# Attention as a three-stage pipeline in fixed TensorE order, with inputs placed early and narrower key blocks at the sides

## The chip, the core and the metric

The program runs on one core of a Trainium2 chip. A core has five engines with an instruction stream each: TensorE (PE, matrix products and transposes), VectorE (DVE), ScalarE (ACT), GpSimd (POOL) and SyncE (SP, which mostly issues DMA transfers). A scheduler in the compiler sets the order of the instructions on each engine; at run time each engine takes its own in that order and waits by semaphores for the others. The metric is the time of one execution on the device in microseconds (us), the median of several runs.

## The reference

Two layers run over 1024 latent tokens (a 16 x 64 grid, width 1024) and 256 context tokens. Each layer has one input projection that feeds three parallel mixers (mLSTM, neighbourhood attention with 8 heads of 64, RG-LRU), one output projection (oproj) over their concatenation, a gated residual, and an MLP. The last layer needs no context output. What the change touches is the neighbourhood attention:

```python
def row_block(r):                       # one row of the grid, 64 queries
    sr = jnp.clip(r - wr // 2, 0, rows - wr)                # 8 key rows
    k_win = k_band[:, :, col_idx]                           # 16 key columns per query
    s_loc = einsum('bqhd,brqchd->bhqrc', q_r, k_win) * scale + bias
    s_ctx = einsum('bqhd,bkhd->bhqk', q_r, kc) * scale      # all 256 context keys
    p = softmax(concatenate([s_loc, s_ctx], axis=-1), axis=-1)
    o = einsum(p_loc, v_win) + einsum(p_ctx, vc)
y_ctx = softmax(qc @ kc * scale) @ vc                       # context tokens, first layer only
x = x + g1 * (concatenate([ym, yn, yl], axis=-1) @ w_out)
```

## The kernel before

All products are fp32 in effect: each operand is split into a high and a low part (`split`, L210 and L211; for weights `load_w`, L200 and L201), and a product is three matmuls (low-high, high-high, high-low). PSUM has 8 banks: three tagged a, two b, one each of c, p and q (`bank`).

A layer runs: input projections of mLSTM and LRU with their scans; then `na_group(0)` and `na_group(1)`, each of which projects K, Q and V for two head pairs, writes them to DRAM token by token (`u_nk`, `u_nq`, `u_nv`) and takes the norms; then the attention stage; then the second half of oproj and the MLP.

**Prep** (`na_prep(hp)`, a generator, one `yield` per step): for a head pair, loads K and Q (`ut`), scales them by their norms on DVE (L684), transposes them on PE (L692, L694), and writes high and low parts as `KH`, `KL`, `QS` (L700 to L706); four DMAs (`KH<-KH`, `KL<-KL`) and one per Q step and head (`QS<-ql`) put the halves on the other 64 partitions. The prep of head pair 0 runs after `na_group(1)`; those of 1 to 3 one step at a time in `side()`.

**Attention** (`na_att`): for each of four head pairs, two units of context queries (layer 0 only) and eight local units: a column block `b` of 16 query columns and a half `g` of 8 query rows, 128 queries, against 32 key columns and 11 (`g = 0`) or 12 (`g = 1`) key rows, 352 or 384 keys, plus 256 context keys. That makes 40 units in layer 0 and 32 in layer 1. A unit, for two heads: score matmuls (L834 local, L838 context) into three a banks; on DVE a fused bias, negation and running minimum for the local keys (L848) and the context keys (L852); Exp on ACT with the row sum into `den` (L855); `side()`; then `softmax_pv`: transposes of the weights (L727), copies of these to SBUF as `PT` (L729, L744 on ACT, L746 on DVE; where the last tile of local keys is 96 wide, three copies for each head instead of one), `den` inverted (L749), spread to 128 x 128 (L751) and transposed by PE (L753), the products with the values `VB` (local) and `VC` (context) (L757), and their scaling into `yr` (ACT copy L865, DVE multiply L866).

**Filler.** The first half of oproj (the rows of mLSTM and LRU; `fill`, `oproj`, matmuls psp at L1363) is handed out by `side()` in pieces of 12 matmuls, paced by `due`; `issue_after` holds a piece behind the scores of the unit. Its inputs `yh` are loaded by `y_load` and split; `ev_half` adds the result to the residual rows in DRAM (`xs`, L1380). Behind the attention, `y_load` and `split` bring the four attention row blocks (`yl`, and `yr` for the last head pair), and the wide oproj takes them (L1363, psa, psp and psq from `xh`, `xlo`; 288 matmuls in layer 0, 192 in layer 1), and adds to `res` (L1464), loaded by SP at L1458. Between them DVE computes modulation vectors from `mr` (L333, L342, L344).

The scheduler may move instructions of different stages past each other on every engine, within what the data, the buffers and `issue_after` allow.

## Time and profile before

| | |
|---|---|
| median of 3 runs | 3132.05 us (3132.0 to 3132.32) |
| the profiled execution | 3124.27 us, its span 3122.5 us |
| mean granted clock of PE, share of full speed | 0.988 |
| PE busy | 3020.2 us, 97% of the span |
| DVE busy | 1900.0 us, 61% |
| ACT busy | 1128.4 us, 36% |

A busy share is the share of the span in which an engine ran an instruction. The attention stage of layer 0 lies at about 510 to 755 us and its wide oproj ends near 805; in layer 1 it is 2130 to 2347, and 2386.

### The profile page before, as it was taken

The page shows a single profiled execution, that of the slowest core. Times are in us where ns is not written, and L with a number is a line of the kernel's source. Part 1 is how long each engine was busy: PE and PEld are TensorE (multiplying, and loading weights), DVE is VectorE, ACT ScalarE, POOL GpSimd, SP SyncE. Part 2 cuts the span into 40 slices and gives each one's busy share as a digit, 9 for nine tenths or more (in the row PEclk, how much of TensorE's full clock was granted, in tenths as well). Part 3 has the DMA queues.
Part 4 walks back from the last instruction along what each step waited for, and adds up shares of the span by engine and source line. Part 5 has one row for each costly group of instructions (what it writes and reads, how often), then busy time and mean ns, then how long its engine had stood idle before and what let it go on. Part 6 is the DMA issues. An engine that isn't in the chain of part 4 may idle for free.

```text
span 3122.5 us, 47474 instructions
## 1 busy us (share of the span) xinstructions
PE 3020.2 (97%) x18250; PEld 2558.1 (82%) x18250; DVE 1900.0 (61%) x4318; ACT 1128.4 (36%) x2011; POOL 291.0 (9%) x252
## 2 busy tenths in 40 slices
PE   7999998999899999999999999998899999999999
PEld 6888898778788888887778889997787777887877
DVE  5757655787977667455444574765787444444444
ACT  4632223574421222233222453234564222332222
POOL 0410000222200000010000511002222000000000
PEclk8999999999999999999999999999999999999999
DMA  9624567765233444233323632347753332333233
GB/s 272 216 73 144 171 190 199 226 169 178 68 115 105 126 124 125 75 108 101 95 88 94 175 123 82 100 131 219 219 172 110 95 95 89 99 116 91 92 96 93
DMA packets 531098, 410.73 MB, mean 132 GB/s; under 512 B 27580, under 2 KB 496536, under 8 KB 530872
## 3 DMA queue, kind: packets, MB, share of 16 engines
q1 hardware_dynamic: 519448, 387.41, 41.9%
q0 software_dynamic: 8576, 15.00, 1.5%
q10 hardware_dynamic: 2848, 5.28, 0.5%
q8 instruction: 144, 2.36, 0.3%
q14 instruction: 82, 0.67, 0.1%
HBM read 339.72 MB, written 67.53 MB: 130 GB/s over the span
## 4 chain that ended last, share of the span: by engine, by line
PE 70%; DVE 11%; DMA 10%; issue 2%; ACT 2%; SPq 1%; POOL 0%; ACTq 0%; DVEq 0%; POOLq 0%
PE psa L468 14%; PE psa L1515 13%; PE psq L468 5%; PE psp L468 5%; PE psp L1515 4%; DMA mr<-in_w_mod_dram 4%; PE psq L1515 4%; PE psp L483 4%; PE psq L483 3%; PE psp L1363 3%; DVE ma L344 3%; PE psc L757 2%; PE psb L727 1%; PE psa L1363 1%; PE psa L834 1%
## 5 line engine op out<-in xcount | busy, mean ns | idle before, releaser
L200 ACT ACTIVATE wh<-wr 128x1024 fp32r<-128x1024 f32 (+3 forms) x356 | 361.8, 1021 | 929.7 <-PE psa L1515 296.3
L201 DVE TENSOR_TENSOR wl<-wr,wh 128x1024 fp32r<-128x1024 f32 (+3 forms) x356 | 424.5, 1196 | 380.6 <-ACT wh L200 374.3
L468 PE MATMUL psa<-xlo,wh 128*128 128x512 f32 (+1 forms) x856 | 319.5, 373 | 2.2 <-DVE xlo L444 2.1
L468 PE MATMUL psa<-xh,wh 128*128 128x512 f32 (+1 forms) x856 | 318.8, 373 | 2.4 <-ACT xh L443 2.4
L468 PE MATMUL psa<-xh,wl 128*128 128x512 f32 (+1 forms) x856 | 319.3, 373 | 1.4 <-DVE wl L201 1.4
L1515 PE MATMUL psa<-hl,wh 128*128 128x512 f32 (+1 forms) x768 | 286.1, 373 | 1.3 <-DVE hl L211 1.3
L1515 PE MATMUL psa<-hh,wh 128*128 128x512 f32 (+1 forms) x768 | 284.6, 376 | 0.6 <-ACT wh L200 0.5
L1515 PE MATMUL psa<-hh,wl 128*128 128x512 f32 (+1 forms) x768 | 278.1, 373 | 0.6 <-DVE wl L201 0.6
L1519 DVE SCALAR_TENSOR_TENSOR res<-psa,modt,res 128x512 f32<-128x512 f32 (+1 forms) x192 | 130.9, 693 | 165.8 <-PE psa L1515 165.6
L468 PEld LDWEIGHTS psa<-xlo,wh 128*128 128x128 f32 x856 | 161.6, 189 | 33.4 <-DVE xlo L444 2.9
L468 PEld LDWEIGHTS psa<-xh,wh 128*128 128x128 f32 x856 | 161.5, 189 | 33.4 <-ACT xh L443 2.8
L468 PEld LDWEIGHTS psa<-xh,wl 128*128 128x128 f32 x856 | 161.6, 189 | 32.5 <-DVE wl L201 2.2
L409 POOL TENSOR_TENSOR acc<-acc,nsq 128x512 f32<-128x512 f32 (+1 forms) x56 | 80.3, 1446 | 1020.6 <-ACT nsq L408 970.7
L210 ACT ACTIVATE hh<-rl 128x512 fp32r<-128x512 f32 (+1 forms) x160 | 93.5, 589 | 225.0 <-DVE rl L1491 225.0
L1515 PEld LDWEIGHTS psa<-hh,wh 128*128 128x128 f32 x768 | 144.5, 188 | 34.8 <-ACT wh L200 8.9
L483 PE MATMUL psp<-wl,xh 128*128 128x256 f32 (+1 forms) x560 | 163.1, 291 | 5.9 <-DVE wl L201 5.8
L1515 PEld LDWEIGHTS psa<-hh,wl 128*128 128x128 f32 x768 | 144.5, 188 | 28.6 <-DVE wl L201 1.5
L1515 PEld LDWEIGHTS psa<-hl,wh 128*128 128x128 f32 x768 | 144.6, 188 | 27.8 <-DVE hl L211 1.5
L483 PE MATMUL psp<-wh,xh 128*128 128x256 f32 (+1 forms) x560 | 162.2, 290 | 2.5 <-ACT wh L200 2.4
L483 PE MATMUL psq<-wh,xh 128*128 128x256 f32 (+1 forms) x560 | 162.7, 290 | 1.4 <-ACT usq L641 0.8
L483 PE MATMUL psq<-wl,xh 128*128 128x256 f32 (+1 forms) x560 | 160.9, 287 | 0.0
L483 PE MATMUL psq<-wh,xlo 128*128 128x256 f32 (+1 forms) x560 | 160.2, 286 | 0.0
(409 smaller groups left out, 7342.4 us busy)
## 6 DMA issues: line engine op xcount, KB each, us to landing
wr<-in_w_mlp_dram SPq DMA_DIRECT2D x256, 512.0 KB
mr<-in_w_mod_dram SPq DMA_DIRECT2D x92, 512.0 KB
wr<-in_w_in_dram SPq DMA_DIRECT2D x48, 512.0 KB
tab<-T_d SPq DMA_DIRECT2D x48, 384.0 KB
T_d<-E_d POOLq DMA_DIRECT2D x48, 256.0 KB, 6.5
ab<-row_d SPq DMA_DIRECT2D x36, 256.0 KB
xT_d<-res SPq DMA_DIRECT2D x4, 2048.0 KB
wr<-in_w_out_dram SPq DMA_DIRECT2D x32, 256.0 KB
```

The source lines that it names most:

```text
L200: act.activation(hi[:, a:b], raw[:, a:b], AF.Copy)
L201: dve.tensor_sub(lo[:, a:b], raw[:, a:b], hi[:, a:b].bitcast(F32))
L210: act.activation(hi, src32, AF.Copy)
L344: dve.scalar_tensor_tensor(a, raw[:, k], s[:, k], a, op0=OP.mult, op1=OP.add)
L409: pool.tensor_add(acc[bi], acc[bi], sq[:, :n])
L468: m = pe.matmul(t[:, :n], w[a][:, k, :], X[bi][b][:, k, :], start=(i == 0), stop=(i == 23))
L483: m = pe.matmul(t[:, :cols], X[bi][b][:, half * 4 + k, o:o + P], ws[half][a][:, k, :], start=(i == 0), stop=(i == 23))
L727: pe.transpose(t[:w, j * P:(j + 1) * P], S[e][:, o:o + w], permT)
L757: pe.matmul(to[64 * e:64 * e + 64, :P], vals[i][:w, 64 * e:64 * e + 64], PT[:w, e, i], start=(i == 0), stop=(i == nt - 1))
L1363: pe.matmul(t[:, :n], w[a][:, k, cc * P:(cc + 1) * P], Y[bi][b][:, k], start=(i == 0), stop=(i == 11))
L1515: m = pe.matmul(t[:, :n], w[a][:, k, cc * P:(cc + 1) * P], H[bi, k][b], start=(i == 0), stop=(i == 3 * GH - 1))
L1519: dve.scalar_tensor_tensor(xr[bi][:, ct], t[:, :n], G2[:, ct, v:v + 1], xr[bi][:, ct], op0=OP.mult, op1=OP.add)
```

## The change

1. On PE, the instructions issued while `pinned[0]` is set, which is the whole attention stage, stay in program order. `issue_after` with the anchors is gone there.
2. `na_att` becomes `na_units`, a generator of units of three parts. One iteration of the new loop runs the scores of unit u, a slot of filler, one prep step of the next head pair, the transposes and copies of unit u-1, the values of unit u-2, and a second slot. Two more iterations drain it. The filler yields after every four matmuls instead of twelve.
3. The prep of head pair 0 runs between the Q and the V projection of `na_group(1)`. The pool of the filler's inputs (`yp`) is opened ahead of `na_group(1)`. Some buffers change: `VB` 3 to 2, `VC` 1 to 2, `xs` 3 to 2; the keys and queries of odd head pairs lie in another pool.
4. Side blocks (b = 0, 3) take 24 key columns, centre blocks 32, and all units 12 key rows: 288 or 384 local keys.
5. The transposed weights leave PSUM in three copies per local unit: 512 and 256 wide on ACT, 512 wide on DVE.
6. `rb` comes from one reciprocal of `den` broadcast to 128 x 128, instead of a reciprocal of 128 x 2 and a broadcast copy.

```diff
+    pinned = [False]
+
+    def in_order(op):
+        def issue(*a, **k):
+            ins = op(*a, **k)
+            return tc.keep_in_program_order(ins) if pinned[0] else ins
+        return issue
+
+    pe = SimpleNamespace(matmul=in_order(nc.tensor.matmul), transpose=in_order(nc.tensor.transpose))
...
-        def na_group(grp):
+        def na_group(grp, between=()):
             na_proj(grp, C_NK, u_nk[l], ALLT, nssq["k"])
             na_proj(grp, C_NQ, u_nq[l], QT, nssq["q"])
+            phase(f"na_prep{l}")
+            run(between)
+            phase(f"na_inB{l}")
             na_proj(grp, C_NV, u_nv[l], ALLT, None)
...
+        def transpose_p(npl, S, w, permT):
+
+
+            PT = npl.tile([P, 10, P], F32, name=nm("PT"), tag="PT", bufs=2)
+            tl = [(e, i * w, w) for e in range(2) for i in range(3)] if w else []
+            tl += [(e, 3 * w + i * P, P) for e in range(2) for i in range(2)]
+            o = 10 - len(tl)
+            for a, b, on_dve in ((0, 4, False), (4, 6, False), (6, 10, bool(w))):
+                if a < o:
+                    continue
                 t = bank("bbq")
-                for j, (e, i) in enumerate(gr):
-                    o, w = tiles[i]
-                    pe.transpose(t[:w, j * P:(j + 1) * P], S[e][:, o:o + w], permT)
-                if len(gr) == 2:
-                    act.activation(PT[:, :, 4], t[:, 0:2 * P].rearrange("p (k q) -> p k q", q=P), AF.Copy)
-                    continue
-                if nt == 2:
-                    act.activation(PT[:, :, 0:2], t.rearrange("p (e k q) -> p e k q", e=2, q=P), AF.Copy)
-                    continue
-                e = gi
-
-                j = 0
-                while j < 4:
-                    j2 = j
-                    w = tiles[j][1]
-                    while j2 < 4 and tiles[j2][1] == w:
-                        j2 += 1
-                    src = t[:w, j * P:j2 * P].rearrange("p (k q) -> p k q", q=P)
-                    if e == 0:
-                        act.activation(PT[:w, e, j:j2], src, AF.Copy)
-                    else:
-                        dve.tensor_copy(PT[:w, e, j:j2], src)
-                    j = j2
-
-            dve.reciprocal(den, den)
+                h = tl[a - o][2]
+                for j in range(a, b):
+                    e, c, _ = tl[j - o]
+                    pe.transpose(t[:h, (j - a) * P:(j - a + 1) * P], S[e][:, c:c + h], permT)
+                src = t[:h, 0:(b - a) * P].rearrange("p (k q) -> p k q", q=P)
+                if on_dve:
+                    dve.tensor_copy(PT[:h, a:b], src)
+                else:
+                    act.activation(PT[:h, a:b], src, AF.Copy)
+            return PT
...
+        def values_p(npl, PT, den, w, loc, vc, permT, ydst):
+
+
             rb_ = npl.tile([P, 2, 64], F32, name=nm("rb"), tag="rb", bufs=2)
-            dve.tensor_copy(rb_, den.unsqueeze(2).to_broadcast([P, 2, 64]))
+            dve.reciprocal(rb_, den.unsqueeze(2).to_broadcast([P, 2, 64]))
...
+                    cw = (24, 32, 32, 24)[b]
+                    kc = (0, 8, 24, 40)[b]
+                    to = 8 if b == 3 else 0
+                    w = 4 * cw
+                    nl = 3 * w
...
-                        nr = 11 if g == 0 else 12
-                        nl = nr * 32
...
+                                pe.matmul(tl[:, :nl].rearrange("p (r c) -> p r c", c=cw), QS[e][:, qo:qo + P],
+                                          kv[:, r0:r0 + 12, kc:kc + cw], start=(i == 0), stop=(i == 1))
...
+        yh_cm = tc.tile_pool(name=f"yh_{l}", bufs=1, reuse_waits="tile")
+        yp = yh_cm.__enter__()
+        na_group(1, preps[0])
...
+                                if not wide and i in (4, 8):
+                                    yield
...
-                        if len(anchors) > 30:
-                            with tc.issue_after(anchors[-1 - 0]):
-                                next(filler, None)
...
+            pinned[0] = True
+            one = two = None
+            phase(f"na_att{l}")
+            for u in itertools.chain(all_units(), (None, None)):
+                if u:
+                    u[0]()
+                slot_()
+                phase(f"na_prep{l}")
+                next(side_[0], None)
                 phase(f"na_att{l}")
-                yr = yk.tile([P, NTOK], F32, name=nm("yr"), tag="yr")
-                na_att(hp, npl, stk[hp], yr, side)
-                if 0 <= hp < 3:
-                    run(preps[hp + 1])
+                if one:
+                    one[1]()
+                if two:
+                    two[2]()
+                slot_()
+                phase(f"na_att{l}")
+                one, two = u, one
...
+            pinned[0] = False
+        yh_cm.__exit__(None, None, None)
         ns_cm.__exit__(None, None, None)
```

The places at which the order changes, engine by engine (names as the program gives them, with a number for the buffer where it helps; `x4` is four alike). First PE in layer 0, a stretch of local units before the change; psp is the filler, psa the scores, psb and psq the transposes, psc the values:

```order
L1363 MATMUL psp_6629<-yh_5935,wl_6545 128x512
L1363 MATMUL psp_6629<-yh_5935,wh_6544 128x512
L1363 MATMUL psp_6629<-yh_5936,wh_6544 128x512
L1363 MATMUL psp_6629<-yh_5935,wl_6545 128x512
L838 MATMUL psa_6199<-KH_5742,QS_5740 128x256
L838 MATMUL psa_6199<-KL_5744,QS_5740 128x256
L838 MATMUL psa_6199<-KH_5743,QS_5741 128x256
L838 MATMUL psa_6199<-KL_5745,QS_5741 128x256
L753 MATMUL psc_6086<-idj,rb_6084 128x128
L757 MATMUL psc_6086<-PT_6062,VB_6017 64x128 x6
L757 MATMUL psc_6086<-PT_6062,VC_5849 64x128 x4
L727 MATMUL psb_6155<-idj,S_6112 128x128 x4
```

After it, within one iteration; the eight score rows of the newest unit stand just ahead of these:

```order
L102 MATMUL psp_6258<-yh_5890,wl_5926 128x512
L102 MATMUL psp_6258<-yh_5890,wh_5925 128x512
L102 MATMUL psp_6258<-yh_5891,wh_5925 128x512
L102 MATMUL psp_6258<-yh_5890,wl_5926 128x512
L102 MATMUL psq_6353<-idj,S_6246 128x128 x3
L102 MATMUL psq_6353<-idj,S_6252 128x128
L102 MATMUL psb_6359<-idj,S_6252 128x128 x2
L102 MATMUL psb_6363<-idj,S_6246 128x128 x2
L102 MATMUL psb_6363<-idj,S_6252 128x128 x2
L102 MATMUL psc_6371<-idj,rb_6369 128x128
L102 MATMUL psc_6371<-PT_6278,VB_6145 64x128 x6
L102 MATMUL psc_6371<-PT_6278,VC_5852 64x128 x4
```

A slot of four filler matmuls now stands ahead of the five rows of transposes and another ahead of the next scores, and transposes and values that stand together belong to different units.

DVE in layer 0, about three head pairs in, before: minima (L848, L852, each with a second row that reads the accumulated value), the broadcast copy `rb` and three `PT` copies:

```order
L848 ISA S_8787,m_1584_8788<-psa_8776,tab_8536 128x384
L848 ISA m_1584_8788 128x1
L848 ISA S_8793,m_1587_8794<-psa_8779,tab_8539 128x384
L848 ISA m_1587_8794 128x1
L852 ISA S_8787,m_1585_8789<-psa_8775,zcol,m_1584_8788 128x256
L852 ISA m_1585_8789 128x1
L852 ISA S_8793,m_1588_8795<-psa_8775,zcol,m_1587_8794 128x256
L852 ISA m_1588_8795 128x1
L751 COPY rb_8759<-den_8707 128x128
L746 COPY PT_8737<-psb_8746 128x256
L746 COPY PT_8737<-psb_8746 96x128
L746 COPY PT_8737<-psb_8746 128x128
```

After, L885 and L889 are the minima, L748 the `PT` copy, L757 the new reciprocal, L902 the multiply:

```order
L885 ISA S_8575,m_1559_8576<-psa_8564,tab_8404 128x384
L885 ISA m_1559_8576 128x1
L885 ISA S_8581,m_1562_8582<-psa_8567,tab_8407 128x384
L885 ISA m_1562_8582 128x1
L889 ISA S_8575,m_1560_8577<-psa_8563,zcol,m_1559_8576 128x256
L889 ISA m_1560_8577 128x1
L889 ISA S_8581,m_1563_8583<-psa_8563,zcol,m_1562_8582 128x256
L889 ISA m_1563_8583 128x1
L748 COPY PT_8591<-psb_8602 128x512
L757 RECIPROCAL rb_8765<-den_8574 128x128
L902 TENSOR_TENSOR yr_8155<-yr_8155,psc_8610 128x8x16
```

The reciprocal of a unit (its `den` is that of `S_8575` and `S_8581` here) now stands behind its minima and one copy, ahead of the multiply of an older unit.

SP at the end of layer 0's stage, before; two more `yl` loads of head pairs 1 and 2 stand three and four rows ahead of these:

```order
L1344 DMA yl_9043<-yT_d_86 128x512
L1344 DMA yl_9047<-yT_d_86 128x256
L1458 DMA res_9070<-xT_d 128x2x256
L1458 DMA res_9071<-xT_d 128x2x512
L1458 DMA res_9070<-xT_d 128x2x256
L1458 DMA res_9071<-xT_d 128x2x512
L1458 DMA res_9070<-xT_d 128x2x256
L1458 DMA res_9071<-xT_d 128x2x512
L1458 DMA res_9070<-xT_d 128x2x256
L1344 DMA yl_9051<-yT_d_86 128x512
L1458 DMA res_9071<-xT_d 128x2x512
L1344 DMA yl_9055<-yT_d_86 128x512
```

After:

```order
L1504 DMA res_8970<-xT_d 128x2x256
L1504 DMA res_8971<-xT_d 128x2x512
L1413 DMA xT_d<-xs_8851 128x512
L208 DMA wr_9198<-in_w_out_dram 128x4x256
L1504 DMA res_8972<-xT_d 128x2x512 x4
L344 DMA mr_9648<-in_w_mod_dram 128x8x128
L1373 DMA yl_8935<-yT_d_86 128x256
L1373 DMA yl_8939<-yT_d_86 128x512
L1373 DMA yl_8943<-yT_d_86 128x512
L1373 DMA yl_8947<-yT_d_86 128x256
L1373 DMA yl_8951<-yT_d_86 128x512
L1373 DMA yl_8955<-yT_d_86 128x512
```

The six `yl` loads moved behind all `res` loads and `mr`. On ACT and DVE all splits of attention rows now stand behind the last unit's output, where before some stood ahead of it, and on PE all wide matmuls stand behind the last values matmul.

## Rows read from the trace of the kernel before

**Rows 1.** Windows: start:end, length, busy us (count) per engine, PEclk, DMA share, GB/s.

```profile
510.00:755.00 245.00, 224.18 (x1809) 190.38 (x1807) 185.36 (x581) 142.66 (x367) 45.44 (x24) 0.96 0.69 197
2130.00:2347.00 217.00, 195.25 (x1536) 159.61 (x1536) 168.01 (x505) 125.36 (x312) 54.72 (x29) 0.97 0.73 213
738.00:755.00 17.00, 17.00 (x154) 14.64 (x150) 7.42 (x18) 4.66 (x13) 0.00 (x0) 1.00 0.77 270
2330.00:2347.00 17.00, 17.00 (x143) 13.79 (x142) 7.30 (x18) 6.77 (x17) 0.00 (x0) 1.00 0.94 324
2130.00:2160.00 30.00, 20.86 (x95) 15.93 (x95) 17.96 (x36) 10.05 (x22) 16.44 (x9) 0.89 0.97 243
```

**Rows 2.** Windows of oproj matmuls, L1363, at the end of both stages.

```profile
738.00:755.00 17.00, 11.77 (x71) 9.61 (x71) 1.00 0.77 270
755.00:805.00 50.00, 46.10 (x218) 37.15 (x218) 1.00 0.46 142
2330.00:2347.00 17.00, 9.73 (x39) 7.04 (x39) 1.00 0.94 324
2347.00:2386.00 39.00, 37.11 (x155) 28.34 (x153) 1.00 0.33 102
```

**Rows 3.** PE's waits in 510 to 755: us in total, times, longest.

```profile
PE psp L1363 <- DVE xs L1380: 4.9, 2, 2.7
```

**Rows 4.** The end chain at both starts: start us, us, what.

```profile
522.45 4.34 DMA QS<-ql
...
2131.85 7.75 DMA KH<-KH
2139.66 7.22 DMA QS<-ql
```

**Rows 5.** DVE groups by shape, 508 to 760: busy us, mean ns.

```profile
L852 DVE CUSTOM_DVE_ANT_0 S<-psa,zcol,m 128x256 f32<-128x256 f32 x64 | 28.8, 475 | 0.1
...
L848 DVE CUSTOM_DVE_ANT_0 S<-psa,tab 128x384 f32<-128x384 f32 x32 | 16.9, 551 | 2.1 <-PE psa L834 2.0
...
L848 DVE CUSTOM_DVE_ANT_0 S<-psa,tab 128x352 f32<-128x352 f32 x32 | 15.8, 515 | 1.9 <-PE psb L727 1.5 <-issue 0.3
...
L751 DVE COPY rb<-den 128x128 f32<-128x128 f32 x40 | 15.1, 378 | 2.6 <-PE psc L753 2.1
...
L746 DVE COPY PT<-psb 128x512 f32<-128x512 f32 x12 | 8.2, 686 | 1.8 <-PE psc L757 1.1 <-PE psb L727 0.7
...
L852 DVE DVE_READ_ACCUMULATOR2_ANT m<- 128x1 f32 x64 | 5.1, 80 | 0.0
...
L746 DVE COPY PT<-psb 128x256 f32<-128x256 f32 x12 | 5.0, 418 | 2.5 <-PE psc L757 2.1 <-PE psb L727 0.4
...
L746 DVE COPY PT<-psb 96x128 f32<-96x128 f32 x12 | 3.3, 276 | 0.0
```

**Rows 6.** DVE, the broadcast copy in 2128 to 2350.

```profile
L751 DVE COPY rb<-den 128x128 f32<-128x128 f32 x32 | 14.1, 442 | 3.5 <-PE psc L753 2.6
```

**Rows 7.** Single lines over the whole span: ns min/median/max.

```profile
L749 DVE RECIPROCAL den<-den x72: 143/156/167, 522.6 to 2330.9; 128x2 f32<-128x2 f32 x72
...
L1286 DVE RECIPROCAL rc<-dn x36: 145/178/180, 302.9 to 2073.3; 128x4 f32<-128x4 f32 x36
...
L751 DVE COPY rb<-den x72: 204/226/1761, 522.8 to 2338.1; 128x128 f32<-128x128 f32 x72
```

**Rows 8.** ACT groups by shape, 508 to 760.

```profile
L855 ACT ACTIVATE S<-S,m 128x640 f32<-128x640 f32 x32 | 26.3, 824 | 12.7 <-DVE m L852 12.7
...
L855 ACT ACTIVATION_READ_ACCUMULATOR S<-S,m 128x1 f32 x64 | 12.1, 188 | 0.0
```

**Rows 9.** The chain that led to the start of layer 0: a load of mixer rows.

```profile
503.75 3.89 DMA yl<-yT_d
```

**Rows 10.** PE groups by shape, 738 to 805: two widths of one line.

```profile
L1363 PE MATMUL psa<-xh,wl 128*128 128x512 f32 x36 | 14.3, 398 | 0.0
...
L1363 PE MATMUL psa<-xh,wh 128*128 128x256 f32 x20 | 5.7, 288 | 0.0
```

More of the change, by code (lines that the diff above doesn't have):

```diff
@@ L770, in na_att, with unit, scores, turn_ @@
             uv = u_nv[l]
             sp.dma_start(VC, uv[0:NCTX, hp * P:(hp + 1) * P].rearrange("(t p) c -> p t c", p=P))
+            def unit(score, w, loc, permT, yd, end):
+                st = SimpleNamespace()
+                def scores():
+                    st.S, st.den = score()
+                def turn_():
+                    st.PT = transpose_p(npl, st.S, w, permT)
+                def values():
+                    values_p(npl, st.PT, st.den, w, loc, VC, permT, yd)
+                    if end:
+                        end()
+                return scores, turn_, values
@@ L866, in yd @@
                             dve.tensor_mul(dst, dst, r.rearrange("p (r c) -> p r c", r=8))
[L868 to L878 removed]
+                        yield unit(score, w, [VB[:, i + g] for i in range(3)], flip, yd,
+                                   store if (b, g) == (3, 1) else None)
         with tc.tile_pool(name=f"m1_{l}", bufs=1, reuse_waits="tile") as m1:
@@ L1389, in fill @@
                     y_load(Yh, part, 0, yp)
+                    for _ in range(LAG if n_ else 0):
+                        yield
                     for _ in oproj(Yh, part, 0, False, ev_half):
@@ L1392, in fill, with slot_ @@
                         phase(f"oproj{l}")
+            LAG = 4
             filler = fill()
-            n_side = 4 * (8 if last else 10)
-            pace = {"fill": sum(8 * len(p_) for p_ in parts), "mod": len(modq), "at": 0}
-            def due(key):
-                i = pace["at"]
-                return (i + 1) * pace[key] // n_side - i * pace[key] // n_side
+            n_slots = 2 * 4 * (8 if last else 10)
+            n_fill = sum(24 * len(p_) for p_ in parts) + LAG
+            at = [0]
+            def slot_():
+                i = at[0]
+                at[0] += 1
+                for _ in range(min(i + 1, n_slots) * n_fill // n_slots - min(i, n_slots) * n_fill // n_slots):
+                    next(filler, None)
             crm = [npl.tile([P, 768], F32, name=nm("crm"), tag="crm", bufs=3) for _ in range(3)]
```

211 lines of the change are left out of this document (97 added, 114 removed).

## The prediction

> **What bounds the kernel now.** I read the page's clock and busy slices first, then windows over each layer's attention stage and the oproj behind it, then who waits for whom there, then durations by shape. TensorE (PE) is the engine to follow. In layer 0 it is busy for 224.18 us of the 245 from 510 to 755, in layer 1 for 195.25 of 217, at a mean granted clock of 0.96 and 0.97 [rows 1]: about 42 us stand idle, and the low clock stretches another 15 or so. The idle is not one wait: the longest single entry of layer 0's waits is 4.9 us of filler matmuls behind the evictions `xs` [rows 3]. Layer 1 loses most at its start: in 2130 to 2160 PE works 20.86 of 30 us at a clock of 0.89 [rows 1], while the end chain goes through two copies of keys and queries by DMA, 7.75 and 7.22 us; layer 0 has one of 4.34 us there [rows 4]. VectorE (DVE) is busy for 185.36 and 168.01 us of the same windows [rows 1], so a gain for PE ends where DVE fills up.
>
> I count each layer from its start of attention to the end of its wide oproj: 510 to 805 and 2130 to 2386, 551 us together. That is 72 units plus the oproj. After the change there are 42 and 34 iterations (each layer drains two), so all prices below are per iteration, over 76.
>
> **PE's own price.** Busy time at the full clock is 224.18 x 0.96 = 215.2 and 195.25 x 0.97 = 189.4. Of these 11.77 and 9.73 us are wide oproj matmuls that ran before the last unit [rows 1, 2]. Left for units, filler and prep: 203.4 + 179.7 = 383.1 us. The change of key columns removes 1024 score columns per head pair (sides: two blocks, two g, four matmuls, 64 or 96 columns less each, 1280; centre: 256 more), 8192 in all; a column costs (398 - 288)/256 = 0.43 ns between two widths [rows 10], so 3.5 us. PE needs 379.6 us, **4.99 per iteration**, if it never waits. Cutting the filler into pieces of four matmuls changes their order, not their number.
>
> **DVE's price.** 353.4 us busy, of which 7.42 and 7.30 lie in the last 17 us of each stage [rows 1], where much of the work is the splits for the wide oproj, which go behind the stage now; I take 10 out: 343.4. Then:
> The small RECIPROCAL (128x2, 156 ns) and the broadcast copy (0.378 us on average in layer 0, 0.442 in layer 1) go, and one RECIPROCAL of 128x128 comes, 72 times [rows 5 to 7]. No row shows that shape. From below: as a copy of 128x128, median 226 ns. From above: the two small shapes are 156 ns for two elements and 178 for four, 11 ns an element by medians; by their slowest (167, 180) 6.5. With 8.5 in between, 0.156 + 126 x 0.0085 = 1.23 us. I take 1.23, since the nearest rows are reciprocals, and a slope shows in them. The sum: +72 x (1.23 - 0.156) = +77.3, minus 40 x 0.378 + 32 x 0.442 = 29.2.
> PT copies: 32 units of g = 0 had three pieces on DVE (0.418, and two of 0.276) and get one of 0.686: -32 x 0.284 = -9.1 [rows 5]. ScalarE (ACT) also loses two per unit, which matters little.
> Score minima: 4096 columns less at (551 - 515)/32 = 1.1 ns: -4.5 [rows 5].
> Together 377.9 us, **4.97 per iteration**: DVE is now as long as PE.
>
> The Trainium skill, page "VectorE: DVE Perf Modes", section "First, the fixed hardware budget", says that Reciprocal is an iterative divide with a repeat count of 8. The small shapes' slope agrees in kind; no run here shows the large shape. Taken as eight steps of about one nanosecond each (an estimate from that page), 128 elements would be some 1.1 us and the sum 9 us smaller than by my 1.23.
>
> **The wait that comes new.** In the changed order RECIPROCAL stands on DVE right behind its own unit's second minimum and one PT copy, and it needs the Exp of both heads. An Exp is 0.824 + 0.188 us [rows 8]; the first starts as the first head's minimum ends, the second minimum takes 0.475 + 0.080 [rows 5], so the second Exp ends 2.02 - 0.56 = 1.47 us after DVE's last minimum. The PT copy covers 0.69; 0.78 is left, and everything behind it on DVE (the multiply `yr`, the next unit's minima, hence PE's score banks) waits. The order of DVE shows only that copy between in 24 of 64 local units, nothing in 5, and evictions or prep steps that cover the rest in 35; ACT's order puts a PT copy between the two Exps in some 15, for which I add 4 us. 24 x 0.78 + 5 x 1.47 + 4 = 30 us, **0.40 per iteration**. Bounds: 0 (hidden by PE's slower iterations) to 1.1 (a copy between the Exps always). I take 5.37 per iteration, 408.1 us.
>
> **Start.** Prep of head pair 0 now stands before the V projection's end, so the copies of [rows 4] land under PE's projection matmuls. I cost it at nothing; without that cover it is 4.34 in layer 0 and 7.75 + 7.22 in layer 1 again, 19 us. VC and VB still load after the last V store, but the values matmuls come two iterations, over 10 us, later.
>
> **The tail of layer 0 gets worse.** Before, wide matmuls ran between the last units (11.77 us of them before 755) and 46.10 us behind [rows 2], 57.9 in all. After, all twelve splits of attention rows stand behind the last unit on ACT and DVE, and on SP's queue the six `yl` loads of the second and third head pairs stand behind twelve `res` loads (5 MB) and `mr` (0.5 MB). They go out from some 3 us before the last unit's end, at the 270 to 324 GB/s that these stretches moved [rows 1] 17 us or more, and a `yl` load alone took 3.89 [rows 9]: the second half of the contraction can start about 17 us after the last unit. PE has 2.5 us of waiting for splits, then about five banks of six matmuls, some 5 us; it stalls for about 10. So 2.5 + 57.9 + 10 = 70 us behind the last unit (bounds 60 and 80). Layer 1 keeps its interleaving: 9.73 + 37.11 = 46.8 us [rows 2].
>
> **Sum.** 408.1 + 70 + 46.8 = 524.9 against 551: -26 us. The profiled execution took 3124.27 us (span 3122.5), the median of the runs 3132.05; I subtract from the median, the same work in 7.8 us more: **3106 us**. The gain is gone at (551 - 116.8)/76 = 5.71 us per iteration.
>
> **The rivals.**
> Fast reciprocal: at 0.226 us DVE falls by 72 us to 4.02 per iteration, the waits disappear behind PE, and PE runs at 5.1 (0.1 for uneven iterations): -47 us, 3085. For it: copies of that shape; against: the slope of the two small reciprocals. 0.22.
> Nothing gained: PE's idle time only moves, from filler behind evictions to scores behind minima, at 5.63 to 5.79 per iteration, or 5.5 with a layer 0 tail of 85 us. In layer 1 DVE is already busy for 168.01 of 217 us [rows 1]. 0.12: 3126 to 3138.
> Slower: the pinned order lets PE not take filler work when the next unit is late, so a DVE wait of 1.1 us per iteration (second Exp held up by a PT copy on ACT, which waits for PE's transposes, which wait behind scores) goes onto the path whole: 4.97 + 1.1 = 6.07, 461 + 117 = 578, +27 us, 3159. It decides from a wait of 0.74 on. For it: before, filler could slip past; against: three stages leave an iteration between a copy and its use. 0.16.
> The change not doing what it says (prep still late): 19 us of the gain gone, 3125; inside the first case's upper end.
>
> **How the numbers follow.** The forecast, 0.50, has its own range 3090 to 3125. With the fast reciprocal (0.22) below and the other two (0.12, 0.16) above, 3082 to 3137 leaves out about a tenth below and somewhat more above. A change of 0.2%, 6.3 us, is about what a measurement of this kernel can tell from none. Faster 0.72, same 0.12, slower 0.16.
>
> **What the profile after would show.** Right: RECIPROCAL 128x128 near 1.2 us; DVE over 85% busy in the stage; DVE idle in front of RECIPROCAL, released by ACT's Exp; a PE gap of about 10 us some 10 us after layer 0's last values matmul, released by splits of `yl`; no DMA of keys or queries in the start of either stage. Wrong: a reciprocal under 0.4 us (then 3085), PE waiting for score banks every iteration for over 0.7 us (then no gain), or no gap in layer 0's tail (10 us better).

## The result, and the profile after

The changed kernel takes 3212.55 us (3210.13 to 3213.61, 4 runs) against 3132.03: slower, at a ratio of 1.0258 [1.024, 1.0275]. Its profiled execution takes 3212.32 us, 88.1 more than that of the kernel before. Ratios below are to the kernel before, timed beside it on the same chip; differences between kernels are taken from ratios (0.001 is 3.1 us).

Windows of the changed kernel: start:end, length, busy us (count) of PE, PEld, DVE, ACT, POOL, then PEclk, DMA share, GB/s. The two stages from first scores to last values, the start of layer 1's, a stretch with prep, the last units of layer 0 (no prep left), and the tail behind them:

```profile
514.00:792.00 278.00, 223.35 (x1735) 190.34 (x1733) 188.99 (x489) 130.53 (x321) 44.26 (x24) 0.89 0.55 156
2185.00:2433.00 248.00, 197.41 (x1519) 166.85 (x1518) 169.00 (x431) 117.17 (x274) 53.15 (x30) 0.90 0.60 172
2185.00:2215.00 30.00, 13.24 (x69) 10.76 (x69) 15.40 (x38) 10.43 (x24) 20.59 (x12) 0.77 0.67 188
575.00:635.00 60.00, 43.20 (x321) 36.86 (x322) 35.95 (x91) 24.90 (x64) 10.78 (x6) 0.83 0.60 162
755.00:792.00 37.00, 36.30 (x326) 31.14 (x324) 27.69 (x73) 19.16 (x47) 3.23 (x2) 1.00 0.49 161
792.00:805.00 13.00, 3.04 (x17) 2.18 (x15) 3.63 (x7) 2.96 (x7) 0.00 (x0) 0.72 1.02 356
805.00:820.00 15.00, 14.13 (x69) 12.34 (x70) 13.31 (x35) 6.69 (x12) 2.49 (x2) 0.79 0.28 81
820.00:862.00 42.00, 42.00 (x211) 34.98 (x211) 33.00 (x67) 17.34 (x27) 20.11 (x18) 1.00 0.29 89
```

Against [rows 1], the stages grew from 245 and 217 us (their starts' gaps within) to 278 and 248. Busy time at the granted clock gives 223.35 x 0.89 + 197.41 x 0.90 = 376.5 us of TensorE work, where the prediction had 379.6. So no work was added: TensorE stood idle for 54.65 + 50.59 = 105 us instead of 42, and the clock, at 0.83 in the stretch with prep and 1.00 behind it, cost 44 us instead of some 15. Of the 88 us, 33 and 31 lie in the two stages and 21 in layer 0's tail, where from the last values to the start of the last `res` of the wide oproj it takes 73.1 us instead of 52.0. The stretch at 755 shows what the pipeline does undisturbed: TensorE is busy for 36.30 of 37 us.

TensorE's waits in layer 0's stage (us in total, times, longest), where [rows 3] had 4.9 behind `xs` at the top:

```profile
PE psq L102 <- DVE ql L719: 18.5, 3, 8.0
PE psb L102 <- ACT PT L750: 8.1, 7, 2.2
PE psq L102 <- DVE KL L714: 7.9, 2, 4.0
PE psa L102 <- DMA KL<-KL: 6.5, 1, 6.5
PE psp L102 <- DVE xs L1412: 5.1, 6, 1.6
```

and in layer 1's:

```profile
PE psb L102 <- ACT PT L750: 14.4, 10, 3.1
PE psa L102 <- DVE m L885: 11.9, 1, 11.9
PE psq L102 <- DVE KL L714: 10.0, 2, 5.4
PE psq L102 <- DVE ql L719: 8.3, 2, 4.4
```

Some 70 of the 105 us are a PSUM bank that TensorE cannot have yet, because one of prep's low parts (`ql`, `KL`) or a copy of weights (`PT`) still has to be read out of it. DVE's waits in layer 0's stage:

```profile
DVE ut L697 <- DMA ut<-u_nq: 18.8, 7, 5.2
...
DVE rb L757 <- ACT S L892: 10.6, 14, 1.4
DVE ut L697 <- DMA ut<-u_nk: 9.3, 7, 3.2
DVE ql L719 <- ACT QS L718: 8.1, 8, 2.0
```

And one of these stretches in the end chain, start us, us, what: a load of `ut` that lands late, the multiply, a low part, and only then TensorE's next transposes into that bank.

```profile
588.66 3.22 DMA ut<-u_nk
...
591.90 0.69 DVE ut L697
...
592.62 0.44 DVE KL L714
...
593.20 1.09 PE psq L102 x4
594.29 2.54 PE psc L102 x21
```

The start of layer 1, in the end chain, where [rows 4] had copies of keys and queries:

```profile
2187.19 4.81 DMA VB<-u_nv
...
2193.04 4.75 DMA ut<-u_nk
2197.88 0.41 DVE ut L697
```

Those copies are gone from it, but a value tile, loaded behind the last store of V, and the first `ut` of the next head pair stand there now, and TensorE is busy for 13.24 of the first 30 us at a clock of 0.77; [rows 1] had 20.86 at 0.89. Taking `ut` away does not cure this, though. With no loads in prep, and no copies in later prep (a run below), TensorE waits there for the minima all the same:

```profile
PE psa L102 <- DVE m L885: 11.0, 2, 10.0
```

and in the end chain of the run without later prep GpSimd stands in front of the first local minimum: it builds the masks `crm` and adds them to the bias tables `tab`, which that minimum reads.

```profile
2107.01 4.21 POOL crm L1444 x3
...
2112.94 2.96 POOL crm L1447 x2
...
2116.45 3.58 POOL tab L844 x2
...
2120.05 0.46 DVE S L885
```

The first local minimum comes 13.2 us behind the first scores there, and 13.7 us in the changed kernel. In the kernel before, GpSimd began the same work at 2128.87, under the copies of keys and queries, and the first scores came at 2144.89.

The reciprocal, ns min/median/max (its relations in [rows 7]):

```profile
L757 DVE RECIPROCAL rb<-den x72: 941/952/955, 519.6 to 2422.0; 128x128 f32<-128x128 f32 x72
```

An iteration, taken from one unit's first score matmul to the next unit's, splits by whether prep transposes ran in it. Means in us, from the instructions of the trace; busy is the time in which the engine ran an instruction. All kernels but the changed one are runs from below:

| kernel, layer | with prep: number, length, DVE busy, ACT busy | without: number, length, DVE, ACT |
|---|---|---|
| changed, 0 | 18, **8.76**, 5.39, 3.73 | 21, **5.23**, 4.07, 2.79 |
| changed, 1 | 15, **9.96**, 6.07, 4.10 | 16, **5.24**, 4.31, 3.05 |
| no loads in prep, 0 | 18, 7.39, 5.60, 3.71 | 21, 5.15, 4.02, 2.80 |
| no loads in prep, 1 | 15, 9.15, 6.32, 4.11 | 16, 5.19, 4.25, 3.05 |
| no copies in prep, 0 | 18, 4.89, 4.13, 2.51 | 21, 5.25, 4.13, 2.91 |
| no copies in prep, 1 | 15, 6.45, 5.08, 2.99 | 16, 5.19, 4.14, 2.93 |
| separate banks, 0 | 18, 8.28, 5.55, 3.71 | 21, 6.38, 4.16, 2.87 |
| separate banks, 1 | 15, 8.55, 5.97, 4.04 | 16, 6.85, 4.67, 3.17 |

Without prep the changed kernel's iteration is close to the forecast mean (5.37). With prep it takes nearly twice that, and no engine is busy for more than 67% of it (TensorE 5.86 of 8.76 us and 6.65 of 9.96). Prep iterations are not alike either. In layer 0's last two head pairs with prep the three steps for K take 6.0 us on average, beside the small context units, and the three for Q 11.6 us, among local units alone. In layer 1, which has no context units, the full-width K steps of the last two such head pairs take 11.5 us.

Layer 0's tail is as forecast. TensorE's waits in 792 to 870:

```profile
PE psa L102 <- ACT xh L221: 10.8, 2, 10.1
```

The gap of 10.1 us lies behind the first 15 wide matmuls and in front of those on the late `yl` loads; the granted clock is 0.72 and 0.79 from 792 to 820, means between its levels of 2.4 and 1.2 GHz, and back at 1.00 from 820. The wide oproj ends near 862, 70 us behind the last values at 792.

### The profile page after: what moved, and what is told of

It reads as the page before. It is cut to its first block, busy times and chain, and to the rows that moved or that the text cites. A ratio compares the mean times of both kernels' runs of the same rounds, so it can differ in the third digit from the quotient of the medians.

```text
span 3210.4 us, 47255 instructions
## 1 busy us (share of the span) xinstructions
PE 3034.3 (95%) x18250; PEld 2573.1 (80%) x18250; DVE 1920.8 (60%) x4182; ACT 1120.3 (35%) x1947; POOL 279.7 (9%) x252
## 4 chain that ended last, share of the span: by engine, by line
PE 69%; DVE 11%; DMA 10%; ACT 3%; issue 2%; SPq 1%; ACTq 0%; DVEq 0%
PE psa L102 30%; PE psp L102 17%; PE psq L102 14%; PE psb L102 5%; DMA mr<-in_w_mod_dram 5%; PE psc L102 3%; DVE ma L355 3%; DMA ut<-u_nk 1%; DVE wl L212 1%; DMA ut<-u_nq 1%; DMA ab<-row_d 1%; DVE res L1565 1%; DMA yl<-yT_d 1%; ACT S L892 1%; DVE hl L222 1%
## 5 line engine op out<-in xcount | busy, mean ns | idle before, releaser
L102 PE MATMUL psa<-xh,wh 128*128 128x512 f32 (+1 forms) x972 | 360.2, 372 | 12.3 <-ACT xh L221 10.8
L102 PE MATMUL psa<-xlo,wh 128*128 128x512 f32 (+1 forms) x972 | 361.4, 372 | 1.3 <-DVE xlo L455 1.3
L102 PE MATMUL psa<-xh,wl 128*128 128x512 f32 (+1 forms) x972 | 360.6, 372 | 1.4 <-DVE wl L212 1.4
L102 PEld LDWEIGHTS psa<-xh,wh 128*128 128x128 f32 x972 | 183.3, 189 | 48.1 <-ACT xh L221 11.5
L102 PEld LDWEIGHTS psa<-xlo,wh 128*128 128x128 f32 x972 | 183.5, 189 | 37.1 <-DVE xlo L455 1.7
L102 PEld LDWEIGHTS psa<-xh,wl 128*128 128x128 f32 x972 | 183.2, 189 | 36.2 <-DVE wl L212 2.2
L420 POOL TENSOR_TENSOR acc<-acc,nsq 128x512 f32<-128x512 f32 (+1 forms) x56 | 72.9, 1310 | 1041.3 <-ACT nsq L419 998.9
```

The lines of the kernel that those rows point to most:

```text
L102: ins = op(*a, **k)
L420: pool.tensor_add(acc[bi], acc[bi], sq[:, :n])
```

## The experiments

Each is the changed kernel with one edit unless the text says otherwise. Theories named in the expectations: A, late prep loads; B, the reciprocal and its wait for Exp; C, the fixed order itself; D, prep's other parts, its banks above all; F, late transfers on SP's queue; G, prep's copies on ACT and VectorE.

**Deeper load buffers.**

```diff
-                    ut = npl.tile([P, 4, P], F32, name=nm("ut"), tag="ut", bufs=2)
+                    ut = npl.tile([P, 4, P], F32, name=nm("ut"), tag="ut", bufs=4)
```

> Only the buffers of the prep loads `ut` change, 2 to 4 (and the filler's load buffers `yl` 3 to 1, to make room), so that a load can go out up to three prep steps ahead of its use instead of one. Theory A (the late `ut` loads: VectorE waits in order for them, and TensorE's fixed order waits behind the prep transposes and the banks they hold): VectorE's 53 us of waiting for `ut` in the two stages falls below 15, the granted clock in the stages rises above 0.95, and the time falls by 50 to 85 us, to 3128 to 3162. Theory B (the reciprocal of 0.95 us and the wait for Exp in front of it): the time stays within 10 us of 3212.

3215.96 us, ratio 1.028 [1.0257, 1.0303]: no gain. DVE's waits in its layer 0 stage:

```profile
DVE ut L697 <- DMA ut<-u_nq: 13.6, 7, 3.6
DVE ut L697 <- DMA ut<-u_nk: 13.4, 4, 6.2
```

27.0 us after 28.1; in layer 1's stage 19.9 after 24.9. The scheduler used the buffers to put load and multiply both earlier (multiplies run up to four prep steps ahead of their transposes, where they ran up to two), so the multiply still stands in DVE's order ahead of its data. The experiment did not take the lateness away and so decides nothing on A; it also took two of the filler's three load buffers.

**The reciprocal undone.**

```diff
-            dve.reciprocal(rb_, den.unsqueeze(2).to_broadcast([P, 2, 64]))
+            dve.reciprocal(den, den)
+            dve.tensor_copy(rb_, den.unsqueeze(2).to_broadcast([P, 2, 64]))
```

> Part 6 alone undone: the reciprocal of 128x2 and the broadcast copy stand in place of the 128x128 reciprocal. Theory B: VectorE loses 72 x (0.95 - 0.16 - 0.3) = 35 us of work, which sets the iteration, so the time falls by 25 to 45 us. Theory A: VectorE is idle for a third of the stages anyway; the time falls by less than 12 us.

3206.61 us, 1.0246 [1.0225, 1.0267]: the interval overlaps that of the changed kernel, at most a few us. Theory B falls: iterations with prep are 8.54 and 10.15 us long, with DVE busy for 5.17 and 5.78.

**No fixed order.**

```diff
-            pinned[0] = True
+            pinned[0] = False
```

> Part 1 alone undone: TensorE's instructions of the attention stage are not held in program order; the scheduler places them. Theory C (the fixed order itself costs the time, whatever is late): the time falls below 3150. Theory A: the loads are as late as before and VectorE waits for them as long (over 40 us in the two stages); TensorE finds other work for a part of it, and the time falls by 10 to 50 us. Theory B: within 15 us of 3212.

3142.29 us, 1.0048 [1.003, 1.0066]: 66 us faster, the bulk of the loss. Theory C holds that far; what the order has to wait for was still open. Some 18 of the 66 us are not the stages' but layer 0's tail, which takes 55.4 us from the last values to the end of the last `res`, instead of 73.8.

**Prep's transposes out of the fixed order.**

```diff
+                pinned[0] = False
                 next(side_[0], None)
+                pinned[0] = True
```

> Only the prep transposes are taken out of the fixed order; scores, transposes of weights, values and filler keep it. Theory A: the scheduler can place the transposes later, but VectorE's order still has the wait for `ut` in it: 0 to 40 us faster. Theory C: with the rest still fixed, within 15 us of 3212. Theory B: within 10 us of 3212.

3153.93 us, 1.008 [1.0058, 1.0101]: 56 us faster, more than either theory gave it. The weights' transposes behind them are held only behind the last prep transpose then, so both may pass the filler of that iteration. Scores, values and filler keep their order at 25 us over the kernel before, and layer 0's tail stays at 73.9 us, so in the stages this gives back at least what freeing all of TensorE did.

**No loads in prep.** `ut` is made from a resident tile by an instruction of the same shape.

```diff
-                    sp.dma_start(ut[:, :n], udr[l][a * P:b * P, hp * P:(hp + 1) * P]
...
-                    dve.tensor_mul(uv, uv, rsn[kd, grp][:, a:b, h0:h0 + 2].unsqueeze(3).to_broadcast([P, n, 2, 64]))
+                    src = idj[:, 0].rearrange("p (e d) -> p e d", e=2).unsqueeze(1).to_broadcast([P, n, 2, 64])
+                    dve.tensor_mul(uv, src, rsn[kd, grp][:, a:b, h0:h0 + 2].unsqueeze(3).to_broadcast([P, n, 2, 64]))
```

> The prep steps do not load `ut`: VectorE makes it from a resident tile, in an instruction of the same shape, so the keys and queries are not the reference's. All else, the fixed order too, is that of the changed kernel. Theory A (VectorE's waits for the loads, seen in the trace, hold up the fixed order): no wait for `ut` is left, TensorE's idle time in the two stages falls from 101 to below 50 us, and the time falls by 60 to 100 us, to 3112 to 3152. Theory D (the prep's other parts: its transposes share three banks with the weights' transposes in a fixed order, and wait for their copies; loads are a bystander): less than 30 us faster.

3172.47 us, 1.0131 [1.0109, 1.0154]: 40 us faster, between the two bands. The late loads are a part, not the whole.

**The multiply on GpSimd**, `dve.tensor_mul(uv, ...)` as `pool.tensor_mul`.

> The multiply of `ut` by the norms runs on GpSimd instead of VectorE; loads, order and all else stay. Theory A: nothing on VectorE waits for a load of `ut` any more, but TensorE's prep transposes still do in the fixed order, and GpSimd needs more than VectorE's 0.7 us: 25 to 70 us faster. Theory D: within 15 us of 3212.

3180.1 us, 1.0158 [1.0133, 1.0182]: 31 us faster. That most of the loads' part is DVE standing still in front of them fits, since TensorE still needs the same loads here; but the edit also takes the multiply itself (0.69 us a step) off DVE, and the two are not separated.

**The prep step last in the iteration** (the step's two lines stand behind the second filler slot).

> The prep step moves from between scores and transposes to the end of the iteration, behind the values and the second filler slot, still in the fixed order. Theory D: the prep's banks are drained while the next scores and filler run, so the weights' transposes wait less for them: 30 to 80 us faster. Theory A: the load gets no more time, since its order goes with the step: within 25 us of 3212.

3168.62 us, 1.0121 [1.0099, 1.0143]: 43 us faster; in layer 0 iterations with prep fall from 8.76 to 7.22 us. I took that for D's banks.

**No prep for head pairs 1 to 3**, which use the keys and queries of head pair 0.

```diff
-                    if hp:
-                        run(preps[hp])
-                    side_[0] = preps[hp + 1] if hp < 3 else iter(())
+                    side_[0] = iter(())
...
-                    yield from na_units(hp, npl, stk[hp], yr_[0])
+                    yield from na_units(hp, npl, stk[0], yr_[0])
```

> Head pairs 1 to 3 use the keys and queries of head pair 0, so 30 of the 40 prep steps and their loads, transposes, copies and DMAs are left out. Both theories: iterations as dense as those of the last head pair, 5.0 to 5.7 us, so 76 x (6.92 - 5.35) = 119 us faster, 90 to 150; what is less than that is due to something that is not prep (the fixed order of the three stages alone, or the reciprocal).

3069.95 us, 0.98 [0.9775, 0.9824]: 143 us faster. The three stages in fixed order are sound by themselves; the loss needs prep in them. (Left out are 33 of 44 steps, six a head pair in layer 0 and five in layer 1.)

**Separate banks.**

```diff
-                    t = bank("b" if hp < 1 else "bbq")
+                    t = bank("b" if hp < 1 else "q")
...
-                t = bank("bbq")
+                t = bank("b")
```

> Only the PSUM banks change: the prep transposes use bank q alone, the weights' transposes the two banks b, where both took b, b, q in turn. Theory D (the third group of weights' transposes lands in the bank of the prep step and waits for its whole drain, ql or KL on VectorE, in the fixed order): TensorE's waits for ql and KL, 47 us in the two stages, nearly vanish, and the time falls by 35 to 80 us. Theory A (late loads alone): within 15 us of 3212.

3228.46 us, 1.0307 [1.0292, 1.0323]: slower still, by 15 us. TensorE's waits in its layer 0 stage:

```profile
PE psb L102 <- ACT PT L750: 39.5, 32, 4.1
...
PE psq L102 <- DVE ql L719: 1.6, 1, 1.6
```

The wait for `ql` fell from 18.5 to 1.6 us as D said, and the time did not: ACT's copies `PT`, 8.1 before, now hold TensorE for 39.5. I took this for proof that the shared bank was only where the delay showed. The table above says otherwise: the iterations with prep became 30 us shorter in all (18 x 0.48 + 15 x 1.41), and those without prep 50 us longer (5.23 and 5.24 to 6.38 and 6.85), since two banks serve the weights' transposes that had three, and `PT` holds TensorE 32 times instead of 7. So the edit brought a cost of its own that hides a gain near D's lower bound of 35, and D is not refuted by it.

**The filler ends earlier**: `n_slots` less by 14.

> Only the pace of the filler changes: its last matmuls run 7 iterations before the end of a stage instead of in the last one. If the gap of 10 us and the low clock behind layer 0's last unit come from inputs that lie in the memory of the filler's inputs or behind them in line, the first wide matmuls now run between the last units and layer 0's tail shrinks by 10 to 20 us; the prep iterations get fuller by a fifth of their filler, for plus or minus 5. In all 5 to 25 us faster. If the loads alone hold the tail, under 5.

3222.34 us, 1.0289 [1.027, 1.0307]: no gain. Between layer 0's last values and its last `res` of the wide oproj there are 53.1 us instead of 73.1, as meant, but its stage took 296.3 instead of 278.0.

**Four together, and with the step last.** Separate banks, multiply on GpSimd, three `ut` buffers, earlier filler; then also the step's place.

> Separate banks, the multiply of `ut` on GpSimd, three `ut` buffers (filler load buffers 3 to 2) and the earlier filler together, all else as in the changed kernel. If A and D each hold a part of the loss and the rest of the three-stage order is sound (the run without prep took 3070): 3090 to 3125, which is faster than the kernel before. If the causes overlap (one wait behind the other): about 3140 to 3165.

3193.57 us, 1.0197 [1.018, 1.0214]. 19 us faster than the changed kernel, where the banks' +15, the multiply's -31 and the filler's +10 make -6 and the third buffer may have added some. The large gain that the causes together should have freed is not there in the time; but iterations without prep are again longer, at 5.94 and 6.27 us against 5.48 and 5.30 with the earlier filler alone, and those with prep fall to 7.10 and 8.64. The two banks cost here too, so the bands of this expectation decide little.

> The same as the run with all four, and the prep step at the end of the iteration. With separate banks the place of the step should matter less: within 12 us of that run. If the place still matters, the prep transposes wait for their input (`ut` through GpSimd), and half an iteration more of time for it makes it 12 to 30 us faster.

3182.61 us, 1.0166 [1.0144, 1.0188]: 10 us better, within the first band. Iterations with prep are down to 6.62 and 7.96 us, those without at 6.03 and 6.73.

**No transfers in prep**: no loads, and GpSimd writes zeros (`pool.memset`) where the DMAs put the other halves of keys and queries.

> The prep steps keep their work on TensorE, VectorE and ACT, but neither load `ut` nor copy keys and queries to the other partitions by DMA (GpSimd writes zeros there; the result is not the reference's). Theory F (late transfers on SP's queue, prep's own above all, hold up the fixed order): near the run without prep plus prep's own work, 3085 to 3120. Theory G (prep's copies on ACT and VectorE, a chain of four in each step, in the middle of a fixed order): little better than without the loads (3172): 3150 to 3175.

3175.26 us, 1.0133 [1.0115, 1.015]: the same as without loads alone. Theory F falls for prep's own copies by DMA.

**And no residual rows**: the filler's evictions neither load nor store as well.

> As the run without prep's transfers, and the filler's evictions neither load nor store the residual rows (VectorE's instruction stays), so SP has no store to wait for in the stages. Theory F with the evictions' stores as the thing that SP waits for: 20 to 50 us faster again, 3065 to 3095. Theory G: above 3140. If it equals the run without prep's transfers, evictions only delayed what is gone there.

3178.78 us, 1.0144 [1.0125, 1.0163]: the same again. What is left of the loss, about 45 us over the kernel before, has none of these transfers in it. The end chain there, in an iteration with prep:

```profile
605.95 0.45 PE psq L102 x4
...
606.42 0.68 ACT QS L717
607.10 0.75 ACT PT L749 x2
607.85 1.62 ACT S L891 x4
...
609.50 0.69 ACT QS L717
...
610.21 0.77 DVE ql L718
...
611.11 0.63 PE psq L102 x4
```

This is the mechanism in one view. TensorE has run four transposes by 606.4 and gets its next bank at 611.1. In between stand ACT's first `QS`, two `PT` copies and the Exps of another unit, the second `QS` behind them, and the `ql` on DVE that needs it.

**Residual rows on GpSimd's queue** (`sp.dma_start` in `ev_half` as `pool.dma_start`).

> Loads and stores of the residual rows for the filler's evictions go out on GpSimd's queue instead of SP's, nothing else changes. Theory F: SP, which waited about 65 us in layer 0's stage for these, sends prep's loads and the value tiles earlier: 25 to 60 us faster. Theory G: within 15 us of 3212.

3214.38 us, 1.026 [1.0238, 1.0283]: no change. SP's waits in layer 0's stage of the changed kernel

```profile
SPq L1413 <- DVE xs L1412: 28.8, 14, 5.7
SPq L1411 <- DMA xT_d<-xs: 24.4, 17, 3.0
```

are gone, and SP waits elsewhere instead (at `tab`, 13.8 us before):

```profile
SPq L841 <- DVE m L885: 37.4, 12, 6.8
SPq L721 <- DVE ql L719: 28.4, 12, 6.2
```

Where SP waits for the evictions makes no difference to the stages.

**No copies in prep.** As the run without loads; for head pairs 1 to 3 a prep step is only its multiply and its transposes, in their place; `QS`, `KH`, `KL`, `ql` and the DMAs behind them are left out, and the keys of head pair 0 serve.

> As the run without loads (3172), and for head pairs 1 to 3 the prep steps keep only their multiply on VectorE and their transposes on TensorE in the fixed order; the copies out of PSUM (ACT and VectorE) and the DMAs behind them are left out, and these head pairs use the keys and queries of the first. Theory G (the chain of ACT and VectorE copies per step, on engines that wait in order for each other, with TensorE's order fixed in front of them): 3080 to 3110, close to the run without prep. If the transposes' place on TensorE is it: above 3140.

3085.36 us, 0.9851 [0.9835, 0.9867]: 88 us faster than without loads alone. Its windows, both stages and the stretch at 575:

```profile
514.00:723.00 209.00, 201.19 (x1736) 173.96 (x1736) 169.21 (x457) 112.74 (x291) 45.35 (x24) 1.00 0.55 169
2113.00:2308.00 195.00, 180.36 (x1520) 156.29 (x1519) 152.89 (x401) 100.14 (x245) 54.82 (x30) 0.96 0.57 173
575.00:635.00 60.00, 59.56 (x524) 52.84 (x523) 50.87 (x145) 32.36 (x84) 12.56 (x7) 1.00 0.63 198
```

TensorE is busy for 59.56 of 60 us at a clock of 1.00, where the changed kernel had 43.20 at 0.83, with the prep transposes in the same fixed place. Theory G holds as far as this run can show it. That it is the copies' place in the orders, and not their work, is argued: freeing the prep transposes gave 56 us back with all of that work in place. In layer 1 iterations with prep are still at 6.45 us, in part for GpSimd's tables at the start (the first takes 12.2). Three things go with the copies here: the hold on the bank that they read, which is D's cause, so G and D are not told apart; a head pair's first scores no longer wait for its own keys (one such wait of 6.5 us in layer 0 above), and the copies' DMAs, worth nothing two runs earlier.

**All three engines in program order**: DVE's and ACT's instructions of the three stages are held as TensorE's.

> VectorE's and ACT's instructions of the three stages are held in program order as TensorE's are (prep and filler work may still move forward). So the reciprocal of a unit stands two iterations behind its Exp, and minima stand in front of prep's copies. Theory G2 (it is the order that the scheduler chose on VectorE and ACT, from its own idea of when things are ready, that clashes with TensorE's fixed order): VectorE's waits for Exp in front of the reciprocal, 20 us, go, and the time falls by 40 to 110 us, to 3100 to 3170. If prep's copies hold up the stages wherever they stand: within 25 us of 3212.

3446.05 us, 1.0997 [1.0979, 1.1015]: 231 us slower, far outside both bands. TensorE's waits in layer 0's stage:

```profile
PE psc L119 <- DVE rb L111: 94.5, 33, 8.8
```

In program order the reciprocal of a unit stands directly in front of TensorE's transpose of it. The scheduler had moved it an iteration forward, to where it waits for Exp but nobody waits for it. So the order chosen on DVE was no fault there; which order of prep's copies would do better stays open.

**A version from the parts that helped**: prep transposes out of the fixed order, multiply on GpSimd, small reciprocal and copy.

> The fixed order without the prep transposes (3154), with the multiply of `ut` on GpSimd (32 us in the changed kernel) and the reciprocal of 128x2 with its copy (6 us). If these add: 3108 to 3125, faster than the kernel before. If freeing the prep transposes has already given back what the late loads cost: 3140 to 3155.

3127.59 us (10 runs), 0.9992 [0.9978, 1.0007]: 83 us faster than the change, the sum of its parts (56 + 31 + 4 = 91) nearly, and level with the kernel before. Layer 0's stage takes 229.0 us, from first scores to last values, against 244.7 before, and its tail gives 20 us back: 72.0 against 52.0. Layer 1's takes 215.7 against 201.6, from first scores that come earlier. Moving the `yl` loads ahead of `res` in such a kernel was not tried.

## Why the prediction was wrong

**What held.** TensorE's price, 376.5 us against 379.6. The tail of layer 0, 70 us with a gap of 10.1 that ends with a split of a late `yl`, in size and in mechanism. DVE's wait for Exp in front of the reciprocal is there, 10.6 + 9.3 us behind ACT's local Exps, where I had 30. The reciprocal was over-sized, 0.952 us against 1.23 (its bounds 0.226 and 1.54), or 6.3 ns for each further element; 72 x 0.28 = 20 us less turns the forecast 377.9 us of DVE work into 358, which is what was measured (188.99 + 169.00). The Trainium skill's page "VectorE: DVE Perf Modes", section "First, the fixed hardware budget", gives a repeat count of 8, from which the estimate in the prediction was about 1.1. The measured 0.952 lies nearer to it than to my 1.23.

The iteration without prep, 5.2 us, agrees with 5.37 partly by luck: 5.37 was a mean with prep's work in it and with DVE as long as PE, and in the undisturbed stretch TensorE sets the pace (36.30 of 37 us) with DVE busy for 27.69. Over both stages DVE is busy for 68%, where I had looked for over 85%.

**The step that failed** is "I take 5.37 per iteration, 408.1 us". The stages took 526 us, 6.92 per iteration; the tails, 70 and 42 us against 70 and 46.8, make no part of the miss. Within that step the fault is in "evictions or prep steps that cover the rest in 35". I added prep's busy time, its loads and copies into a mean over 76 iterations, as work that fills gaps, and gave its waits no term. But prep comes one step per iteration in the first five or six of a head pair, and each step must pass within one iteration through load, multiply, transposes, and a chain that goes from ACT to DVE and back twice (`QS`, `ql`, `QS`, `ql`), on engines that also have two units' Exps, minima and copies in line. Nothing of that is long as work: DVE is busy for 5.4 to 6.1 us and ACT for 3.7 to 4.1 of an iteration that lasts 8.8 to 10.0. Nor is it long in the direct waits of its links (15.3 us of DVE's time for `QS` in both stages, 3.4 of ACT's for `ql`): as the view at 605.95 shows, most of it is standing in line behind the units' own work. The fixed order makes TensorE wait for the end of that chain, for a bank, in the middle of the iteration. In place of cover, prep is the load. (8.76 - 5.23) x 18 + (9.96 - 5.24) x 15 = 134 us, close to what leaving prep out gave (143).

Taken away one after the other, the 143 us are 40 for the loads; 88 for the copies, with the banks that they hold; and 15 for multiply and transposes. Another order of removal could divide them otherwise. With the clock, which was low where TensorE stood still, that is more than the whole forecast gain.

**A second term, the start,** "I cost it at nothing", was also wrong. The copies of head pair 0 did land under the projection, but another delay lay under theirs: GpSimd's `crm` and `tab`, on which the first local minima wait. Moving the scores forward laid it bare: layer 1's first minimum stands 13 us behind its scores with or without prep, and TensorE waits 11.9 us for minima with prep's loads and 11.0 without loads and copies. In the changed kernel `ut` lands last, but little later than the tables. So some 7 of the 134 us, in layer 1's first iteration, are not prep's.

**The rivals.** The slower one (0.16) had the right head, a fixed order that keeps TensorE from filler work when something is late, and a wrong cause: Exp in front of the reciprocal, priced at 27 us; undoing the reciprocal changed almost nothing. That prep's transfers would be late was a rival only for the two starts, at 19 us, and they were 40. "ScalarE (ACT) also loses two per unit, which matters little" hid the other engine of the chain: I never priced ACT per iteration.

**What stays open.** Why ACT's and DVE's orders, which served the kernel before with the same prep steps, cost so much beside the fixed one is shown only by its ends: freeing the prep transposes gives 56 us back, removing the copies 88. Which single crossing of the two orders costs most was not separated, nor how much of the 88 is the bank held (D) and how much the chain that holds it (G): that needs a bank for prep that the weights' transposes do not lose. Parts 4 and 5 and the smaller buffers of part 3 were not undone; in the run without later prep, which has them all, layer 0's iterations take 5.18 us.

## What to carry to other kernels

A mean per iteration over engines hides the iterations that differ: price the heaviest kind of iteration by itself, as a chain through all engines and queues, before an order is fixed. Fixing one engine's order makes every late input of any instruction in it a stall of all; put work with a long chain (a load, then two engines in turn) outside the fixed order (56 us here) or later in the iteration (43 us). When an experiment takes something from one user to give it to another, as the separate banks did, look at the stretches in which the first user is alone before a cause is dropped. More buffers do not make a load early if the reader's place in its own in-order queue moves forward with it. And a delay that is moved away may have covered another, as the copies covered GpSimd's tables.

## What the runs showed of the hardware

A reciprocal of 128x128 takes 941 to 955 ns in 72 executions, with next to no spread, where a broadcast copy of that shape took 204 to 1761 [rows 7]. The granted clock was 0.83 where TensorE was busy for 43.20 of 60 us, and 1.00 for 59.56 of the same 60 in the kernel without copies; behind the gap of 10.1 us in layer 0's tail it was 0.79 over 15 us although TensorE was busy for 14.13 of them. Over the two stages 105 us of idle time went with 44 us of stretched work. The multiply of `ut` takes GpSimd 1.05 us (615 to 1523 ns) where DVE takes 0.69.
